# Even mixer of a two-layer encoder step: scan fronts in pinned steps, Toeplitz blocks in column tiles, a shorter warm-up

## The chip, the cores and the metric

One of the eight cores of a Trainium2 chip. The time is device microseconds from launch to end. Engines: PE (TensorE, matmuls), DVE (VectorE), ACT (ScalarE), POOL (GpSimd), and SP (SyncE), which here only issues DMAs. Each works off its own list of instructions in order and waits on semaphores for the others.

## What is computed

A step of a trunk of two layers over 512 prompt frames and 32 sample frames, 1024 features, f32. Layer 0 has the even mixer: a short gated convolution (A) beside a state space model with complex diagonal (B), both from one projection; layer 1 has attention and spatial gating. Each layer ends in a ConvFFN and a gated embedding. Cut to the even mixer:

```python
z = hn @ W['w_even_in'][j]
gb, gc, xa, u = jnp.split(z, [A_WIDTH, 2 * A_WIDTH, 3 * A_WIDTH], axis=-1)
yc, new_hist = causal_dwconv(gc * xa, hist, W['w_conv_a'][j])
ya = gb * yc
yb, nr, ni = s5_mixer(u, h0r, h0i, ...)   # scan over time, 32 groups x 64 states, then
                                          # y = Re(c h) + d*u; g = gelu(y); g * sigmoid(g @ w_glu)
y = jnp.concatenate([ya, yb], axis=-1) @ W['w_even_out'][j]
```

## The kernel before

Activations stand with features on partitions: 8 tiles of 128 features by 544 columns, in two halves of 256 and 288 columns. Every f32 weight and activation is split into a high and a low part (`wh`, `wl`, `Xh`, `Xl`), so that a product of a 128x128 block is three passes (L131 to L133), and a job (`mm_job`) over eight blocks of K is 24 passes, some 3 us. `prefetch` (L92) keeps four weight units loaded ahead: a DMA on SP, `wh` on ACT (L107), `wl` on DVE (L108). `phase` (L166) runs the jobs of a projection, and after each job calls `run(rate)`, which advances the first generator in `tasks` by `rate` steps (`yield`s); a step that yields True ends that call. The result of a job is consumed `lag` jobs later (`drain`), which frees its PSUM buffer; there are four.

The order of each engine's list is laid out when the kernel is built, by a planner that takes the instructions in the order in which the program writes them, but lets one pass ahead that it estimates to be ready sooner.

`mixer_even` (L518) has two phases. The first makes `u` (four units, `c_u`), with norms and `discretize` beside it (rotations `E`, powers `pw`). The second makes A's three parts (`c_a`: 12 units, two halves, so 24 jobs, two steps a job, lag 2), with `scan` beside it. `scan` (L897) is B in chunks: time is cut in blocks of four frames, M = 137 block columns, and the 16 group pairs go two at a time through eight fronts.

- `prep_g(ch)` (L802): builds `G` for four group pairs on ACT and DVE (one step), transposes it on PE into `Bm` (a second).
- `prep_c` (L780): the output matrices `Cm` for the powers 0 to 4, on DVE (L789, L791), in `Tm`'s space as scratch, then zeroes `Tm`.
- `prep_t(ch)` (L831): the Toeplitz blocks inside a block of four frames, `tp` (L837), four group pairs side by side on 32 partitions; copies into `Tm` (L840, L842), and three DMAs on SP for the shifted copies (L845).
- `front(s)` (L852): input products `v` on PE, rotation (L867 to L870), a scan along time (L875) whose coefficients ACT writes into `sp` (L872), rotation back (L877 to L879). `rt`, `rg`, `sp` and `G` come from one pool of four buffers.
- `back(s)` (L883): output products from `sp` and `Tm` on PE, GELU on ACT (L894).
- `shuffle` (L917): 16 DMAs on SP that bring two column groups back to feature order (L924).

The order in `scan` is `back(s-2)`, `front(s)`, then a preparation; a front is one step. Its 32 steps are all plain. After the phase `GG` is made of the shuffled result (L977, L978), and eight products with `w_glu` follow, then the output projection. Ahead of everything PE runs nine matmuls on zeros (L218).

Of the kernel before, what the change touches and what calls it, by code (L numbers as in the profile page):

```python
# [24 lines left out]
M = 137  # L25
# [15 lines left out]
PC["_n"] = 0  # L41
for _n, _w in (("g_mix_pre", 16), ("g_mix_post", 16), ("g_ffn_pre", 16), ("g_ffn_post", 16),
               ("conv_a", 12), ("hist_a", 8), ("a_re", 16), ("a_im", 16),
               ("log_dt", 16), ("st_re", 16), ("st_im", 16), ("d", 16), ("b_forget", 1),
               ("g_gmlp", 4), ("conv_f", 264)):
    _pc(_n, _w)
NPRM = PC["_n"]
NPRM0 = PC["conv_f"][0]

NCST = 128 + 128 + 32  # L50


def units():
# [18 lines left out]
def trunk_kernel(ctx: ExitStack, tc: tile.TileContext, A: dict):  # L72
    nc = tc.nc
    vec, act, pool_e, pe = nc.vector, nc.scalar, nc.gpsimd, nc.tensor
# [132 lines left out]
    cst = const.tile([128, NCST], F32, tag="cst", name="cst")  # L207
    ident = cst[:, 0:128]
    mask_p = cst[:, 128:256]
    mask_s = cst[:, 256:288]  # L210
    ones = const.tile([128, 1], F32, tag="ones", name="ones")
    vec.memset(ones, 1.0)
    mhalf = const.tile([128, 4], F32, tag="mhalf", name="mhalf")
    zero = const.tile([128, 8], F32, tag="zero", name="zero")
    vec.memset(zero, 0.0)
    warm = mm.tile([128, 512], F32, tag="mm", name="warm")
    for _ in range(9):
        pe.matmul(warm[:, 0:256], zero[:, 0:1].to_broadcast([128, 128]), zero[:, 0:1].to_broadcast([128, 256]),  # L218
                  start=True, stop=True)
    act.activation(mhalf, zero[:, 0:4], AF.Gelu_apprx_tanh)  # L220
# [2 lines left out]
    def P(name, j=0, n=1):  # L223
        o, _ = PC[name]
        return prm[:, o + j:o + j + n]
# [292 lines left out]
    def mixer_even(h):  # L518
        ms = ExitStack()
        s5 = ms.enter_context(tc.tile_pool(name="s5", bufs=1))  # L520
# [259 lines left out]
        def prep_c():  # L780
            ct = Tm.rearrange("p (n i a x) c -> p n i a (x c)", n=2, i=2, a=2)
            ct = ct.rearrange("p n i a (q c) -> p n i a q c", q=16)
            for tau in range(5):
                src = raw[:, 0]
                if tau:
                    t = ct[:, tau % 2]
                    for i in range(2):
                        p_ = pw[:, tau, i][:, None, :, None].to_broadcast([128, 2, 16, 16])
                        vec.tensor_tensor(t[:, i], raw[:, i], p_, op=OP.mult)  # L789
                    src = t[:, 0]  # L790
                    vec.tensor_tensor(src, src, t[:, 1], op=OP.add)  # L791
                for g in range(2):
                    s = slice(g * 64, g * 64 + 64)
                    act.activation(Cm[s, :, :, tau, g * 16:g * 16 + 16], src[s], AF.Copy)
                if tau % 2 == 0:
                    yield
            act.activation(Tm.rearrange("p q s -> p (q s)"), zero[:, 0:1].to_broadcast([128, 2048]), AF.Copy)
            yield

        g3 = {}  # L800

        def prep_g(ch):  # L802
            q0 = 4 * ch
            G = pt([128, 2, 4, 4, 32], "G")
            g3[ch] = s5.tile([128, 2, 4, 32], F32, tag="g3", name="g3", bufs=2)
            act.activation(G.rearrange("p a b c d -> p (a b c d)"),
                           zero[:, 0:1].to_broadcast([128, 1024]), AF.Copy)
            for g in range(2):
                s = slice(g * 64, g * 64 + 64)
                act.activation(G[s, :, :, 3, g * 16:g * 16 + 16], bb[s, 0, ch], AF.Copy)  # L810
            act.activation(g3[ch], G[:, :, :, 3], AF.Copy)
            t = [s5.tile([128, 8, 3, 16], F32, tag="gt", name="gt", bufs=2) for _ in range(2)]
            for i in range(2):
                p_ = pg[:, i, q0:q0 + 4][:, None, :, :, None].to_broadcast([128, 2, 4, 3, 16])
                b_ = bb[:, i, ch][:, :, :, None].to_broadcast([128, 2, 4, 3, 16])
                vec.tensor_tensor(t[i].rearrange("p (r q) j c -> p r q j c", r=2), b_, p_, op=OP.mult)
            vec.tensor_tensor(t[0], t[0], t[1], op=OP.add)
            for g in range(2):
                s = slice(g * 64, g * 64 + 64)
                o = G[s, :, :, 0:3, g * 16:g * 16 + 16].rearrange("p r q j c -> p (r q) j c")  # L820
                act.activation(o, t[0][s], AF.Copy)
            yield
            for r in range(2):
                ps = aux.tile([128, 512], F32, tag="y", name="tb", bufs=2)
                for i in range(4):
                    pe.transpose(ps[:, i * 128:i * 128 + 128],
                                 G[:, r, i].rearrange("p j c -> p (j c)"), ident)
                act.activation(Bm[:, r, q0:q0 + 4].rearrange("p q s -> p (q s)"), ps, AF.Copy)
            yield

        def prep_t(ch):  # L831
            q0 = 4 * ch
            G = g3.pop(ch)
            ps = aux.tile([128, 512], F32, tag="y", name="tp", bufs=2)
            for i in range(4):
                for r in range(2):
                    pe.matmul(ps[0:32, i * 128:i * 128 + 128], G[:, r, i],  # L837
                              Cm[:, r, q0 + i, 0:4].rearrange("p t c -> p (t c)"), start=(r == 0), stop=(r == 1))
            pv = ps[0:32].rearrange("p (q s) -> p q s", q=4)
            act.activation(Tm[0:32, q0:q0 + 4, 32:128], pv[:, :, 32:128], AF.Copy)  # L840
            for i in range(4):
                vec.scalar_tensor_tensor(Tm[0:32, q0 + i, 0:32], ident[0:32, 0:32], P("d", q0 + i)[0:32],  # L842
                                         pv[:, i, 0:32], op0=OP.mult, op1=OP.add)
            for j in range(1, 4):
                nc.sync.dma_start(Tm[j * 32:j * 32 + 32, q0:q0 + 4, j * 32:128], Tm[0:32, q0:q0 + 4, 0:128 - j * 32])  # L845
            yield


# [3 lines left out]
        def front(s):  # L852
            q0 = 2 * s
            U4 = UV["U4"]
            ps = aux.tile([128, 2, 512], F32, tag="v", name="v")
# [8 lines left out]
            cf = sp[:, 2:4].rearrange("p a i m -> p (a i m)")[:, 0:4 * M]  # L864
            cv = cf.rearrange("p (r i m) -> p r i m", r=2, i=2)
            t4 = t.rearrange("p e r (q m) -> p e r q m", q=2)
            vec.tensor_tensor(t, v[:, None].to_broadcast([128, 2, 2, 2 * M]), e, op=OP.mult)  # L867
            vec.tensor_tensor(g[:, 0], t4[:, 0, 0], t4[:, 1, 1], op=OP.add)
            vec.tensor_tensor(g[:, 1], t4[:, 0, 1], t4[:, 1, 0], op=OP.subtract)
            vec.tensor_copy(g[:, 0:2, :, 128], P("st_re", 0, 32).rearrange("p (r q) -> p r q", r=2)[:, :, q0:q0 + 2])  # L870
            for i in range(2):
                act.activation(cv[:, :, i], seg[:, None].to_broadcast([128, 2, M]), AF.Copy, scale=K_["mag4"][:, q0 + i:q0 + i + 1])  # L872
            pool_e.memset(sp[:, 0:2, :, 0:1], 0.0)
            g_ = g.rearrange("p (x r) i m -> p x (r i m)", x=2)
            vec.tensor_tensor_scan(g_[:, 1], cf, g_[:, 0], 0.0, op0=OP.mult, op1=OP.add)  # L875
            w_ = g_[:, 1].rearrange("p (r x) -> p r x", r=2)
            vec.tensor_tensor(t, w_[:, None].to_broadcast([128, 2, 2, 2 * M]), e, op=OP.mult)  # L877
            vec.tensor_tensor(sp[:, 0, :, 1:M + 1], t4[:, 0, 0], t4[:, 1, 1], op=OP.subtract)
            vec.tensor_tensor(sp[:, 1, :, 1:M + 1], t4[:, 0, 1], t4[:, 1, 0], op=OP.add)  # L879
            act.activation(so[:, q0:q0 + 2].rearrange("p q (r c) -> p r q c", r=2), sp[:, 0:2, :, 128:138:9], AF.Copy)  # L880
            SP[s] = sp
# [13 lines left out]
                           AF.Gelu_apprx_tanh)  # L895

        def scan():  # L897
            yield from prep_g(0)
            yield from prep_g(1)
            for s in range(10):  # L900
                if s >= 2:
                    back(s - 2)
                    yield
                if s == 5:
                    shuffle(True, (0, 1))
                if s < 8:
                    front(s)
                    yield
                    if s == 0:
                        yield from prep_c()  # L910
                    if s % 2 == 0:
                        yield from prep_t(s // 2)
                    elif s < 5:
                        yield from prep_g(s // 2 + 2)
            shuffle(True, (2, 3))

        def shuffle(back_, fs):  # L917
# [458 lines left out]
def host_arrays(inp):  # L1376
# [51 lines left out]
    def put(name, a):  # L1428
        o, n = PC[name]
        prm[:, o:o + n] = a  # L1430
# [19 lines left out]
    put("d", np.tile(f["s5_d"][0].reshape(16, 32).T, (4, 1)))  # L1450
# [6 lines left out]
    cst[:, 128:256] = np.where(i[None, :] <= i[:, None], 0.0, NEG)  # L1457
    j = np.arange(32)
    cst[:, 256:288] = np.where(j[None, :] <= (i % 32)[:, None], 0.0, NEG)
    A["cst"] = cst  # L1460

    def gpc(v):
# [56 lines left out]
```

## Time and profile before

| | us |
|---|---|
| median of 3 runs | 1391.64 |
| lowest and highest | 1391.41, 1392.94 |
| profiled execution | 1392.53 |
| its span, first to last instruction | 1390.8 |

| engine | busy us | share of the span |
|---|---|---|
| PE matmul | 1367.2 | 98% |
| DVE | 935.7 | 67% |
| ACT | 657.4 | 47% |
| POOL | 198.3 | 14% |

The times are read from one execution of the program; the even mixer takes the first 170 us of it. A busy PE may still lose time, since matmuls are pipelined: what counts is how far apart their starts are. The profile's page gives the sums; the stretches, the waits and the timelines tell where in the kernel they arise.

### The profile page before, as it was taken

How to read it: one execution, taken by the hardware profiler on the slowest of the kernel's cores; microseconds unless marked ns; L12 is line 12 of the kernel's file. 1: busy time of each engine (PE TensorE's matmuls, PEld its weight loads, DVE VectorE, ACT ScalarE, POOL GpSimd, SP SyncE). 2: the span in 40 equal slices, each digit the busy share in tenths (PEclk: the TensorE clock that was granted, in tenths of full speed). 3: DMA queues.
4: the chain of work that ended last, by engine and by line, in shares of the span. 5: the costliest groups of instructions: out<-in, count | busy, mean ns of one | idle time of the engine just before them, and what ended most of it. 6: DMA issues, size and time to landing. Idle time of an engine off the chain costs nothing.

```text
span 1390.8 us, 27437 instructions
## 1 busy us (share of the span) xinstructions
PE 1367.2 (98%) x10859; PEld 1344.2 (97%) x10859; DVE 935.7 (67%) x1968; ACT 657.4 (47%) x1314; POOL 198.3 (14%) x621
## 2 busy tenths in 40 slices
PE   8899999999999999999999999999999999999998
PEld 8798999999999999999998998999999999999998
DVE  9998738983477546868655555479843676368682
ACT  6653545543344223445547755465433343234451
POOL 1000000431022201300131100012320123013000
PEclk9999999999999999999999999999999999999999
DMA  6322352232312231331332332331223123313321
GB/s 199 94 67 63 117 184 77 77 96 72 122 62 86 97 122 39 105 113 53 99 94 70 117 109 64 108 107 62 92 92 122 46 92 107 99 50 94 100 73 50
DMA packets 49376, 128.26 MB, mean 92 GB/s; under 512 B 8368, under 2 KB 19896, under 8 KB 48992
## 3 DMA queue, kind: packets, MB, share of 16 engines
q1 hardware_dynamic: 47456, 124.35, 28.0%
q0 software_dynamic: 1792, 2.17, 0.7%
q8 instruction: 85, 1.39, 0.4%
q14 instruction: 43, 0.35, 0.1%
HBM read 116.93 MB, written 4.76 MB: 88 GB/s over the span
## 4 chain that ended last, share of the span: by engine, by line
PE 87%; DVE 8%; ACT 2%; SPq 1%; DMA 1%; issue 1%; POOL 0%; ACTq 0%; DVEq 0%
PE ps L131 27%; PE ps L133 27%; PE ps L132 27%; DVE wl L108 1%; SPq L924 1%; PE av L1254 1%; PE rp L307 1%; DVE Xl L327 1%; PE pp L1243 1%; DVE rg L875 1%; DVE rt L877 1%; ACT wh L107 1%; PE sc L1230 1%; DVE y L338 0%; DMA h<-in_x 0%
## 5 line engine op out<-in xcount | busy, mean ns | idle before, releaser
L131 PE MATMUL ps<-Xh,wh 128*128 128x256 f32 (+1 forms) x2512 | 728.1, 290 | 1.8 <-ACT wh L107 1.1
L133 PE MATMUL ps<-Xh,wl 128*128 128x256 f32 (+1 forms) x2512 | 725.5, 289 | 2.0 <-DVE wl L108 2.0
L132 PE MATMUL ps<-Xl,wh 128*128 128x256 f32 (+1 forms) x2512 | 725.6, 289 | 0.8 <-DVE Xl L327 0.5
L131 PEld LDWEIGHTS ps<-Xh,wh 128*128 128x128 f32 x2512 | 473.9, 189 | 4.4 <-ACT wh L107 1.6
L132 PEld LDWEIGHTS ps<-Xl,wh 128*128 128x128 f32 x2512 | 474.7, 189 | 3.0 <-DVE Xl L327 1.2
L133 PEld LDWEIGHTS ps<-Xh,wl 128*128 128x128 f32 x2512 | 473.0, 188 | 2.5 <-DVE wl L108 2.4
L108 DVE TENSOR_TENSOR wl<-raw,wh 128x1024 fp32r<-128x1024 f32 (+2 forms) x214 | 256.9, 1201 | 151.3 <-ACT wh L107 149.5
L107 ACT ACTIVATE wh<-raw 128x1024 fp32r<-128x1024 f32 (+2 forms) x214 | 222.1, 1039 | 248.3 <-PE ps L132 232.9
L131 PE MATMUL ps<-gh,wh 128*128 128x288 f32 (+1 forms) x704 | 203.5, 289 | 0.0
L133 PE MATMUL ps<-gh,wl 128*128 128x288 f32 (+1 forms) x704 | 203.4, 289 | 0.0
L132 PE MATMUL ps<-gl,wh 128*128 128x288 f32 (+1 forms) x704 | 202.5, 288 | 0.0
L132 PEld LDWEIGHTS ps<-gl,wh 128*128 128x128 f32 x704 | 133.5, 190 | 0.0
L131 PEld LDWEIGHTS ps<-gh,wh 128*128 128x128 f32 x704 | 133.0, 189 | 0.0
L133 PEld LDWEIGHTS ps<-gh,wl 128*128 128x128 f32 x704 | 132.9, 189 | 0.0
L278 ACT ACTIVATE t<-U,prm 128x256 f32<-128x256 f32 (+1 forms) x176 | 90.4, 517 | 71.0 <-DVE U L413 67.5
L279 DVE SCALAR_TENSOR_TENSOR t<-U,prm,t 128x256 f32<-128x256 f32 (+1 forms) x176 | 87.2, 498 | 34.9 <-ACT t L278 34.7
L413 DVE TENSOR_TENSOR U<-ps,rB 128x256 f32<-128x256 f32 (+1 forms) x176 | 76.6, 437 | 23.9 <-PE ps L133 19.8
L280 DVE SCALAR_TENSOR_TENSOR t<-U,prm,t 128x256 f32<-128x256 f32 (+1 forms) x176 | 87.5, 501 | 4.5
L416 POOL COPY hca<-U 128x2 f32<-128x2 f32 x88 | 24.3, 277 | 366.2 <-DVE U L413 366.1
L423 ACT ACTIVATE t<-t 128x288 f32<-128x288 f32 (+1 forms) x88 | 37.7, 429 | 81.6 <-DVE t L280 81.5
L439 DVE TENSOR_TENSOR y<-y,ps 128x256 f32<-128x256 f32 (+1 forms) x64 | 27.9, 436 | 62.0 <-PE ps L133 62.0
L429 ACT ACTIVATE gh<-t 128x288 fp32r<-128x288 f32 (+1 forms) x88 | 37.4, 425 | 67.3 <-DVE t L427 67.3
(272 smaller groups left out, 1376.7 us busy)
## 6 DMA issues: line engine op xcount, KB each, us to landing
raw<-in_w_up SPq DMA_DIRECT2D x88, 512.0 KB, 3.4
raw<-in_w_down SPq DMA_DIRECT2D x32, 512.0 KB, 3.4
raw<-in_w_odd_in SPq DMA_DIRECT2D x21, 512.0 KB, 3.6
raw<-in_w_gate SPq DMA_DIRECT2D x16, 512.0 KB, 4.0
raw<-in_w_even_in SPq DMA_DIRECT2D x15, 512.0 KB, 3.7
raw<-in_w_down SPq DMA_DIRECT2D x16, 384.0 KB, 3.1
raw<-in_w_even_out SPq DMA_DIRECT2D x8, 512.0 KB, 4.0
raw<-in_w_odd_out SPq DMA_DIRECT2D x8, 512.0 KB, 3.5
```

What stands on the lines that cost most here:

```text
L107: act.activation(wh[:, k], raw[:, k], AF.Copy)
L108: vec.tensor_tensor(wl[:, k], raw[:, k], wh[:, k], op=OP.subtract)
L131: pe.matmul(ps[:, :n], wh[:, k0 + k, :], h_, start=(i == 0), stop=False)
L132: pe.matmul(ps[:, :n], wh[:, k0 + k, :], l_, start=False, stop=False)
L133: pe.matmul(ps[:, :n], wl[:, k0 + k, :], h_, start=False, stop=(i == last))
L278: act.activation(t, v[2], AF.Copy, scale=w(2))
L279: vec.scalar_tensor_tensor(t, v[1], w(1), t, op0=OP.mult, op1=OP.add)
L280: vec.scalar_tensor_tensor(t, v[0], w(0), t, op0=OP.mult, op1=OP.add)
L413: vec.tensor_tensor(block_view(U, half)[2], like(ps, half), like(rB[half], half), op=OP.mult)
L423: act.activation(t, t, AF.Gelu_apprx_tanh)
L429: act.activation(gh[:, f - f0], g, AF.Copy)
L439: vec.tensor_tensor(yk, yk, ps, op=OP.add)
```

## The change

- A front becomes a generator of three pieces: rotation, scan with the first half of the rotation back, and the rest. `pin` (`tc.keep_in_program_order`) holds an instruction behind the one that the program writes just before it on its engine; it is put on DVE's operations of `prep_c` and `prep_g` and on four of a front.
- `scan` takes four steps a front and advances one list of preparations (`side`) between them; `left` says how many of these must be done ahead of a front. `back(s-2)` now stands behind the scan of front `s`. `back(6)` and `back(7)` are the last two.
- `prep_c` yields after each power from 1 on; the first step of `prep_g` yields True.
- `prep_t` writes the four blocks of a chunk to four column tiles of PE, on 128 partitions of one PSUM tile; two copies into `ts_` take them all, and 16 DMAs carry them into `Tm`, the diagonal included. `d` is laid out to fit (4 columns for 16), and `cst` has 32 columns more.
- The warm-up has seven matmuls for nine.

```diff
-    for _ in range(9):
+    for _ in range(7):
...
             for i in range(2):
...
-                        vec.tensor_tensor(t[:, i], raw[:, i], p_, op=OP.mult)
+                        pin(vec.tensor_tensor(t[:, i], raw[:, i], p_, op=OP.mult))
                     src = t[:, 0]
-                    vec.tensor_tensor(src, src, t[:, 1], op=OP.add)
+                    pin(vec.tensor_tensor(src, src, t[:, 1], op=OP.add))
...
-                if tau % 2 == 0:
+                if tau:
                     yield
...
-            yield
+            yield True
...
-            for i in range(4):
-                for r in range(2):
-                    pe.matmul(ps[0:32, i * 128:i * 128 + 128], G[:, r, i],
-                              Cm[:, r, q0 + i, 0:4].rearrange("p t c -> p (t c)"), start=(r == 0), stop=(r == 1))
-            pv = ps[0:32].rearrange("p (q s) -> p q s", q=4)
-            act.activation(Tm[0:32, q0:q0 + 4, 32:128], pv[:, :, 32:128], AF.Copy)
-            for i in range(4):
-                vec.scalar_tensor_tensor(Tm[0:32, q0 + i, 0:32], ident[0:32, 0:32], P("d", q0 + i)[0:32],
-                                         pv[:, i, 0:32], op0=OP.mult, op1=OP.add)
-            for j in range(1, 4):
-                nc.sync.dma_start(Tm[j * 32:j * 32 + 32, q0:q0 + 4, j * 32:128], Tm[0:32, q0:q0 + 4, 0:128 - j * 32])
+            ts_ = s5.tile([128, 128], F32, tag="ts", name="ts")
+            for r in range(2):
+                for i in range(4):
+                    pe.matmul(ps[32 * i:32 * i + 32, 0:128], G[:, r, i],
+                              Cm[:, r, q0 + i, 0:4].rearrange("p t c -> p (t c)"), start=(r == 0), stop=(r == 1),
+                              tile_position=(0, 32 * i))
+            vec.scalar_tensor_tensor(ts_[:, 0:32], eye4, P("d", ch), ps[:, 0:32], op0=OP.mult, op1=OP.add)
+            act.activation(ts_[:, 32:128], ps[:, 32:128], AF.Copy)
+            for j in range(4):
+                for i in range(4):
+                    nc.sync.dma_start(Tm[j * 32:j * 32 + 32, q0 + i, j * 32:128],
+                                      ts_[32 * i:32 * i + 32, 0:128 - j * 32])
...
             pool_e.memset(sp[:, 0:2, :, 0:1], 0.0)
+            yield
             g_ = g.rearrange("p (x r) i m -> p x (r i m)", x=2)
-            vec.tensor_tensor_scan(g_[:, 1], cf, g_[:, 0], 0.0, op0=OP.mult, op1=OP.add)
+            pin(vec.tensor_tensor_scan(g_[:, 1], cf, g_[:, 0], 0.0, op0=OP.mult, op1=OP.add))
             w_ = g_[:, 1].rearrange("p (r x) -> p r x", r=2)
             vec.tensor_tensor(t, w_[:, None].to_broadcast([128, 2, 2, 2 * M]), e, op=OP.mult)
-            vec.tensor_tensor(sp[:, 0, :, 1:M + 1], t4[:, 0, 0], t4[:, 1, 1], op=OP.subtract)
+            yield
+            pin(vec.tensor_tensor(sp[:, 0, :, 1:M + 1], t4[:, 0, 0], t4[:, 1, 1], op=OP.subtract))
...
+            side = [prep_c(), prep_t(0), prep_g(2), prep_t(1), prep_g(3), prep_t(2), prep_t(3)]
+            left = [0, 0, 1, 3, 5, 5, 6, 6]
+
+            def beside():
+                while side:
+                    try:
+                        return next(side[0])
+                    except StopIteration:
+                        side.pop(0)
+
+            for s in range(8):
+                while 7 - len(side) < left[s]:
+                    yield beside()
+                f = front(s)
+                next(f)
+                yield
+                yield beside()
+                next(f)
+                yield
                 if s >= 2:
                     back(s - 2)
...
+                x = beside()
+                if s == 6:
                     shuffle(True, (0, 1))
...
+                yield x
+                next(f, None)
+            yield
+            while side:
+                beside()
+            back(6)
+            yield
+            back(7)
             shuffle(True, (2, 3))
```

## Rows read from the trace of the kernel before

**Rows 1.** The page: busy time and instructions by engine; the chain, by engine.

```profile
PE 1367.2 (98%) x10859; PEld 1344.2 (97%) x10859; DVE 935.7 (67%) x1968; ACT 657.4 (47%) x1314; POOL 198.3 (14%) x621
...
PE 87%; DVE 8%; ACT 2%; SPq 1%; DMA 1%; issue 1%; POOL 0%; ACTq 0%; DVEq 0%
```

**Rows 2.** Stretches: length; busy PE, PEld, DVE, ACT, POOL; clock; DMA; GB/s.

```profile
38.40:60.00 21.60, 20.31 (x167) 20.01 (x166) 21.60 (x56) 15.06 (x31) 0.11 (x1) 1.00 0.48 129
...
60.00:80.00 20.00, 15.41 (x107) 14.06 (x105) 20.00 (x37) 11.96 (x19) 0.11 (x1) 0.83 0.11 33
...
100.00:120.00 20.00, 17.22 (x138) 16.20 (x137) 14.25 (x28) 8.64 (x22) 0.30 (x3) 1.00 0.22 60
...
140.00:156.10 16.10, 16.10 (x126) 16.10 (x126) 11.60 (x23) 7.76 (x17) 0.00 (x0) 1.00 0.37 112
```

**Rows 3.** PE's waits, 44 to 157 us: total us, times, longest.

```profile
PE tp L837 <- ACT Cm L794: 4.5, 1, 4.5
PE tb L826 <- ACT G L821: 2.9, 3, 1.3
PE yp L893 <- DMA Tm<-Tm: 1.8, 1, 1.8
PE yp L891 <- DVE sp L878: 1.4, 1, 1.4
```

**Rows 4.** Stretches, L837 alone: length; busy PE, PEld; clock; DMA; GB/s.

```profile
66.15:69.73 3.58, 3.54 (x16) 2.60 (x16) 0.50 0.00 0
83.70:85.57 1.87, 1.86 (x16) 1.67 (x16) 1.00 0.00 0
```

**Rows 5.** Timeline of PE, 755 us: start, us, instruction, count.

```profile
755.01 0.88 PE L1254 MATMUL av<-pT,VT 128*64 128x128 f32 x12
755.82 0.33 PE L1230 MATMUL sc<-KA,QA 128*128 128x128 f32 x1
```

**Rows 6.** Timeline of PE at its longest wait.

```profile
66.19 0.63 PE L837 MATMUL tp<-Cm,g 128*32 128x128 f32 x2 [4.48 <-ACT Cm L794]
```

**Rows 7.** DVE by line, 44 to 137 us: count, busy us, mean ns.

```profile
L867 DVE TENSOR_TENSOR rt<-v,E 128x1096 f32<-128x1096 f32 x8 | 10.3, 1289 | 0.0
...
L789 DVE TENSOR_TENSOR Tm<-Bm,pw 128x512 f32<-128x512 f32 x8 | 5.4, 683 | 0.0
...
L878 DVE TENSOR_TENSOR sp<-rt 128x274 f32<-128x274 f32 x8 | 3.5, 436 | 0.1
...
L941 DVE TENSOR_TENSOR gct<-ps,rB 128x256 f32<-128x256 f32 (+1 forms) x7 | 3.0, 423 | 0.0
...
L108 DVE TENSOR_TENSOR wl<-raw,wh 128x1024 fp32r<-128x1024 f32 x7 | 8.5, 1214 | 0.0
```

**Rows 8.** Timeline of SP's queue: start, us, transfer, count.

```profile
101.25 0.33 SPq L106 DMA_DIRECT2D raw<-in_w_even_in  x1
...
112.92 1.88 SPq L845 DMA_DIRECT2D Tm<-Tm  x3
...
132.02 10.31 SPq L924 DMA_DIRECT2D UUh<-UUh  x16
```

**Rows 9.** DMA issues: transfer, count, size, us to landing.

```profile
UUh<-UUh SPq DMA_DIRECT2D x32, 34.2 KB, 1.9
```

**Rows 10.** Timelines of ACT and PE at the end of the scan.

```profile
136.71 0.40 ACT L894 ACTIVATE UUh<-yp 128x274 f32<-128x274 f32 x1 [1.08 <-PE yp L893]
...
145.13 0.66 ACT L977 ACTIVATE GG<-UUh 128x548 fp32r<-128x548 f32 x1 [3.21 <-DMA UUh<-UUh]
...
156.05 0.28 PE L131 MATMUL ps<-GG,wh 128*128 128x274 f32 x1
```

**Rows 11.** Timelines of PE and DVE at the start.

```profile
1.03 6.52 PE L218 MATMUL warm<-zero 128*128 128x256 f32 x18 [1.03 <-DVE zero L215]
...
13.46 0.38 PE L133 MATMUL ps<-Xh,wl 128*128 128x256 f32 x1 [0.86 <-DVE wl L108]
...
7.93 2.65 DVE L327 SCALAR_TENSOR_TENSOR Xl<-h,prm,Xh 128x256 fp32r<-128x256 f32 x6 [0.32 <-ACT Xh L323]
```

More of the change, by code (lines that the diff above doesn't have):

```diff
@@ L43 @@
                ("conv_a", 12), ("hist_a", 8), ("a_re", 16), ("a_im", 16),
-               ("log_dt", 16), ("st_re", 16), ("st_im", 16), ("d", 16), ("b_forget", 1),
+               ("log_dt", 16), ("st_re", 16), ("st_im", 16), ("d", 4), ("b_forget", 1),
                ("g_gmlp", 4), ("conv_f", 264)):
@@ L48 @@
 NPRM0 = PC["conv_f"][0]
-NCST = 128 + 128 + 32
+NCST = 128 + 128 + 32 + 32
 def units():
@@ L210, in trunk_kernel @@
     mask_s = cst[:, 256:288]
+    eye4 = cst[:, 288:320]
     ones = const.tile([128, 1], F32, tag="ones", name="ones")
@@ L794, in prep_c @@
                     act.activation(Cm[s, :, :, tau, g * 16:g * 16 + 16], src[s], AF.Copy)
-                if tau % 2 == 0:
+                if tau:
                     yield
             act.activation(Tm.rearrange("p q s -> p (q s)"), zero[:, 0:1].to_broadcast([128, 2048]), AF.Copy)
-            yield
         g3 = {}
+        pin = tc.keep_in_program_order
         def prep_g(ch):
@@ L815, in prep_g @@
                 b_ = bb[:, i, ch][:, :, :, None].to_broadcast([128, 2, 4, 3, 16])
-                vec.tensor_tensor(t[i].rearrange("p (r q) j c -> p r q j c", r=2), b_, p_, op=OP.mult)
-            vec.tensor_tensor(t[0], t[0], t[1], op=OP.add)
+                pin(vec.tensor_tensor(t[i].rearrange("p (r q) j c -> p r q j c", r=2), b_, p_, op=OP.mult))
+            pin(vec.tensor_tensor(t[0], t[0], t[1], op=OP.add))
             for g in range(2):
@@ L821, in prep_g @@
                 act.activation(o, t[0][s], AF.Copy)
-            yield
+            yield True
             for r in range(2):
@@ L866, in front @@
             t4 = t.rearrange("p e r (q m) -> p e r q m", q=2)
-            vec.tensor_tensor(t, v[:, None].to_broadcast([128, 2, 2, 2 * M]), e, op=OP.mult)
+            pin(vec.tensor_tensor(t, v[:, None].to_broadcast([128, 2, 2, 2 * M]), e, op=OP.mult))
             vec.tensor_tensor(g[:, 0], t4[:, 0, 0], t4[:, 1, 1], op=OP.add)
@@ L899, in scan @@
             yield from prep_g(1)
-            for s in range(10):
+            side = [prep_c(), prep_t(0), prep_g(2), prep_t(1), prep_g(3), prep_t(2), prep_t(3)]
[15 more added lines that the diff above has]
+                yield
                 if s >= 2:
                     back(s - 2)
-                    yield
-                if s == 5:
+                x = beside()
+                if s == 6:
                     shuffle(True, (0, 1))
[L906 to L914, printed above, removed]
+                yield x
[6 more added lines that the diff above has]
+            back(7)
             shuffle(True, (2, 3))
@@ L1449, in host_arrays @@
     put("st_im", gp(f["state_ssm_im"][0, 0]))
-    put("d", np.tile(f["s5_d"][0].reshape(16, 32).T, (4, 1)))
+    put("d", f["s5_d"][0].reshape(4, 128).T)
     prm[:8, PC["b_forget"][0]] = f["b_forget"][0]
@@ L1459, in host_arrays @@
     cst[:, 256:288] = np.where(j[None, :] <= (i % 32)[:, None], 0.0, NEG)
+    cst[:, 288:320] = np.tile(np.eye(32), (4, 1))
     A["cst"] = cst
```

## The prediction

> **What bounds the kernel now.** I read the page first: the share of busy time and the chain of work that ended last. TensorE (PE) is busy for 98% of the span and makes up 87% of the chain [rows 1]. So a microsecond counts only if PE's stream gets shorter or one of its waits does. Next I read busy time by stretch, for the even mixer's second phase alone (38.4 to 156.1 us) [rows 2]. There VectorE (DVE) is busy for all of 21.6 us and then for all of 20 us, while PE loses 4.6 us of the second stretch and its granted clock falls to 0.83, a mean of full (2.4 GHz) and half (1.2 GHz). In the last stretch, 140 to 156.1, PE is busy throughout. So two engines are full in turn: DVE early, PE late. Last I read PE's waits in the phase: 4.5 us for `Cm`, 2.9 us in three waits for `G`, 1.8 us for a transfer into `Tm`, 1.4 us for the last front, 10.6 us in all [rows 3]. That is what better order could return; it is also all of it.
>
> The profiled execution took 1392.53 us, of which 1390.8 are its span; the median of the runs is 1391.64. The other 1.7 us lie around the span and are not touched, so I work out a difference inside the span and put it on the median.
>
> **Toeplitz blocks in column tiles.** Before, a block of four takes 16 passes one after the other, 1.86 us, and 3.54 us in the one case where the clock stood at 0.50 [rows 4]. After, four 32-column tiles take the same passes side by side. The trace has this with two tiles: 12 passes of L1254, also 128 columns of f32, fill 0.81 us from their start to the next instruction [rows 5], so a pair costs about 0.1 and leaving the group 0.2. Four side by side in four rounds: 4 x 0.11 + 0.2 = 0.64. Saved: 4 x (1.86 - 0.64) = 4.9 us, on PE, which is the bound late in the phase. Bounds: only two ever overlap, 8 x 0.1 + 0.2 = 1.0, saves 3.4; none overlap, 0; a price below 0.64 isn't to be had from these rows. I take 4.9, since the pair row shows full overlap.
>
> **Where a run's steps end.** A step of `scan` is advanced twice after each of the phase's 24 jobs, and a step that yields True ends that turn. Two steps of `discretize` are left over at the phase's start. Before, `scan` has 32 steps, none True: 34 steps, so `back(7)` stands after job 17. After, I count 42 steps, four of them True (one in each `prep_g`): `back(7)` stands after job 23. This carries most of what follows. Six jobs of about 3 us that lay behind the scan now lie among it.
>
> **The waits for G, 2.9 us.** `prep_g` now ends its turn, so one whole job always lies between DVE's part and the transposes. I take 2.5 back. Bounds: 0 (the buffer of `G` may be what is late, and it comes from the same four as the fronts') to 2.9.
>
> **The wait for Cm, 4.5 us, and the clock.** The wait itself is a row; the half clock behind it cost 3.54 - 1.86 = 1.7 in that block alone [rows 3, 4]: 6.2 together. PE sat from 61.7 to 66.19 [rows 6]. After, `prep_t(0)` stands two jobs later; a pass of a late job is 0.128 (126 in 16.1 us), a job of 24 is 3.1 [rows 2], so PE would come at 67.9. But power 3 of `prep_c`, the last that this block needs, is now pinned behind front 0, the first half of front 1, and three jobs' consumption. From the rows on DVE: two long operations and smaller ones of the second front's start 1.3 + 2 x 0.44 + 0.1, the end of the first 0.9, six operations of 0.43 for three jobs 2.6, one weight split 1.2, and four operations of `prep_c` that ran ahead of the first front before, 2.7 [rows 7]: about 9.7 us more. Of the last 2.7 I take 1.8 off, since the first front starts sooner without them, as soon as its rotations are done. So `Cm` is ready near 66.1 + 7.9 = 74.0. PE would wait 6.1; the planner can put the ninth job (3.1) in front. Left: 3.0 + 1.7 of clock = 4.7, a gain of 1.5. Bounds: everything goes (6.2) to 3 lost. It is not free that DVE work is pinned: whatever is queued behind a pinned scan on DVE, the consumption of jobs among it, holds PE's PSUM buffers.
>
> **Toeplitz transfers.** Three transfers a block become 16, all on SP's queue, and the diagonal block now goes by SP too; 12 become 64. Before, three take 1.88, and 16 of the shuffle 10.31, so 0.63 each; a weight load, one run a partition, takes 0.33 [rows 8]. The new ones have one run a partition like the load, but 32 partitions like the copies: I take 0.45, with 0.33 and 0.63 as ends. Landing takes 1.9 more [rows 9]. A block is then whole 16 x 0.45 + 1.9 + 0.5 for the two copies = 9.6 us after its matmuls. `back(0)` follows `prep_t(0)` by two jobs (6.2) and the 16 passes of a front and of `prep_g` (1.9, as 16 passes of rows 4), 8.1 us: a wait of 1.5, nearly the present one of 1.8, so 0 here (bounds: 1.8 gained at 0.33, as 7.7 is under 8.1; at 0.63 a wait of 4.4, 2.6 lost). SP's weight loads queue behind, but a weight is loaded four units ahead, so 7 to 10 us stay hidden; without that cover each late unit would stop PE for what is missing. `ts_` is a single buffer: the two writes of `prep_t(3)`, one job after `prep_t(2)`, wait for all of its 16 transfers, on DVE and ScalarE, with a front's scan queued behind. DVE's sixteen small operations become four, a gain of 2 us on an engine with some idle by then: nothing. The last front's wait of 1.4: 0.5 back (bounds 1.4 to -3).
>
> In a sentence apart, the Trainium skill, page "DMA: Bandwidth & Descriptors" (Specifications), gives about 0.6 us as the first-byte latency of the queues that SP uses, and its rules for kernel authors advise one 128-partition transfer over several on parts; the 0.63 rows agree with the first and the 0.33 row does not; by 0.6 the wait above would be 3.9 and the term a loss of about 2.1 instead of 0.
>
> **The end of the scan.** Before, `back(7)` ends at 136.7, its GELU at 137.1, the last transfers are issued by 142.33, the first conversion that needs them starts at 145.13, and PE turns to `GG` at 156.05 without a wait [rows 8, 10]: 19.3 us of jobs cover it, 6.3 jobs, where the written order leaves seven. After, one job (3.1) is left. `back(6)` and `back(7)` now stand in one turn, so all 16 transfers, 10.3, are still to issue: 0.4 + 10.3 + 1.9, less the 1.4 of `back(7)`'s own twelve passes, plus 0.7 for the conversion, so 11.9 from `back(7)`'s end to the first product that needs it. Cover: job 24, 3.1; the first half of the inputs of four products, which don't depend on those transfers, 24 passes, 3.1; what slides behind the waiting backs, 0.7 job as before, 2.2. Left 3.5, and as the clock fell in a wait of 4.5 before, 1.7 again: 5.2 lost. Bounds: 0 (two jobs more slide) to 11.9 - 3.1 + 1.7 = 10.5.
>
> **Warm-up.** Two matmuls less are 4 of 18 passes. Behind them the first job waits on other things: `Xl` comes off DVE until 10.6, and the second job waits for `wl` until 13.46 [rows 11]. Those don't move, so 0. Bounds: 4/18 x 6.5 = 1.4 gained; lost, if the clock opens later, about the same.
>
> **Sum.** -4.9 - 2.5 - 1.5 + 0 - 0.5 + 5.2 + 0 = -4.2. The few columns less of `prm` and more of `cst` go in loads that nothing here waits for. 1391.64 - 4.2 = **1387.4 us**.
>
> **Rivals.**
> 1. *The end is covered*: waits shift jobs behind `back(7)`, or the scan finishes sooner, and the 5.2 shrinks to 0: -9.4, 1382.2 us. For it: before, the planner already slid jobs behind waiting products. Against: DVE was full early, and six jobs' work now stands ahead of the last front on it.
> 2. *A swap*: tiles overlap in pairs only (+1.5) and the end costs 7 (+1.8): -0.9, 1390.7 us. Here the change does, in time, not what it says: one wait for another.
> 3. *SP decides* (slower): at 0.63 a transfer `back(0)` costs 2.6 more, and `prep_t(3)` holds DVE for about 10.1 + 1.9 - 4 = 8 us behind `ts_`. The fronts are one chain on DVE, so I let 6 of them reach the end: -4.2 + 2.6 + 6 = +4.4, 1396.0 us. For it: SP's 0.63 rows. Against: between 100 and 120 us DVE is busy for 14.3 of 20 [rows 2], so it can make some of that up. It decides from about 0.5 us a transfer.
>
> **How the numbers follow.** Forecast 0.40, rival 1 0.22, rival 2 0.19, rival 3 0.19. What a measurement of this kernel can tell from no change is about 0.2%, 2.8 us: the border is 1388.9, close to the forecast, of which I count 0.30 as faster and 0.10 as the same. Faster 0.30 + 0.22 = 0.52; same 0.10 + 0.19 = 0.29; slower 0.19. The forecast's own range is 1384.5 to 1390.5. The range reaches into rivals 1 and 3: 1381 to 1396; half of either's spread lies outside.
>
> **What would show it.** Each Toeplitz block's 16 passes within 0.5 to 0.7 us of PE (else term one is wrong). PE's waits for `G` below 1 us. A wait for `Cm` or for a PSUM buffer near 67 to 75 us, with the clock at half behind it. SP issuing the new transfers at 0.33 to 0.63 each, and whether `back(0)` waits for `Tm`. At the end, an idle PE ahead of the `GG` products for some 4 us, released by the shuffle's last transfers: if there is none, rival 1; if 8 or more, rival 2 or 3. The prediction fails above all if the planner's order moves `back(7)` far from job 23.

## The result and the profile after

The changed kernel takes 1400.49 us (median of 5 runs, 1398.02 to 1402.45), the kernel before 1391.64 in the same comparison (1389.78 to 1393.72). The ratio is 1.0059, 95% interval 1.0041 to 1.0077: 0.6% slower. The profiled execution took 1398.38 us with a span of 1396.6; it is one of the quicker ones, so its trace shows 5.8 us of span more than before, not the whole 8.85. Matched matmul by matmul from the end, the two traces are 7.3 us apart at 185 to 220 us, where the even mixer is done. Then 1.6 us of this go, and over the 1,140 us that follow 5.7 stay, within 0.2. The 1.6 us are no work of the change: in the profiled execution of the kernel before, PE ran the same jobs at half clock at 231 to 234.5 us, behind a wait of 0.5 us that both kernels have. A stretch of each (columns as in rows 2), before and after:

```profile
232.00:234.00 2.00, 2.00 (x11) 2.00 (x11) 2.00 (x7) 1.29 (x3) 1.34 (x4) 0.50 0.00 0
```

```profile
238.00:240.00 2.00, 2.00 (x19) 2.00 (x19) 1.47 (x6) 1.24 (x3) 1.24 (x5) 1.00 0.00 0
```

So the loss arises in the even mixer, and there it is 7.3 us in this pair of traces.

The page's chain, by engine and by line, beside rows 1:

```profile
PE 85%; DVE 8%; SPq 3%; ACT 2%; DMA 2%; issue 1%; POOL 0%; DVEq 0%; ACTq 0%
PE ps L131 27%; PE ps L133 27%; PE ps L132 27%; DVE wl L108 2%; SPq L846 2%; PE av L1276 1%; SPq L946 1%; DVE Xl L328 1%; PE rp L308 1%; DMA raw<-in_w_glu 1%; PE pp L1265 1%; ACT wh L107 1%; DVE rg L878 1%; PE sc L1252 1%; DVE rt L880 0%
```

SP's share went from 1 to 3%, and the line that brought it is L846: the 64 new transfers are themselves on the path that sets the end, and with them the two loads of `w_glu` (at 112.2 and 145.5 us).

Stretches (columns as in rows 2). PE loses its time in three places: 60 to 80 (3.9 us, 4.6 before), 120 to 140 (2.2, 1.4 before), and above all 140 to 156.1 (7.1), where it was busy throughout before:

```profile
60.00:80.00 20.00, 16.13 (x127) 15.03 (x126) 19.92 (x34) 11.04 (x20) 0.10 (x1) 0.91 0.17 53
...
120.00:140.00 20.00, 17.85 (x142) 17.47 (x142) 16.95 (x29) 7.86 (x20) 0.21 (x2) 1.00 0.11 25
140.00:156.10 16.10, 9.03 (x71) 8.80 (x69) 12.36 (x21) 6.08 (x15) 0.10 (x1) 0.88 0.41 126
...
156.00:162.00 6.00, 5.59 (x25) 5.62 (x26) 5.79 (x12) 2.50 (x6) 0.00 (x0) 0.50 0.17 40
```

The last of these rows shows the clock at its lower level (1.2 GHz) behind that loss: PE works at half speed from 156.4 to 162.6 us.

PE's waits, 44 to 178 us (rows 3 is the same view of before): total us, times, longest.

```profile
PE yp L895 <- DVE sp L882: 9.1, 2, 7.4
PE v L860 <- DVE rt L869: 2.8, 2, 2.4
PE tb L827 <- ACT G L822: 2.7, 3, 1.1
PE yp L895 <- ACT Cm L795: 1.5, 1, 1.5
PE ps L131 <- ACT GG L999: 1.1, 1, 1.1
PE yp L897 <- DMA Tm<-ts: 0.9, 1, 0.9
```

With two of 0.4, and 1.8 in front of the output projection behind 178 us, they make 20.7 us, against 10.6 before plus 0.8 at the same place behind 157 us, so 9.3 more. Work at the half clock costs 2.6 more: 1.7 behind the wait at 70 us and 3.1 here, against 2.2 before. The column tiles give 4.9 back (below). 9.3 + 2.6 - 4.9 = 7.0 of the 7.3 us; 0.3 is unexplained.

The Toeplitz blocks alone (L839), columns as in rows 4. The last row holds two blocks:

```profile
70.50:73.00 2.50, 1.08 (x16) 0.59 (x16) 0.50 0.02 7
98.90:99.70 0.80, 0.64 (x16) 0.38 (x16) 1.00 0.00 0
111.40:112.60 1.20, 1.13 (x32) 0.75 (x32) 1.00 0.28 34
```

So 0.64 us where it was 1.86, at full clock: four tiles do run side by side.

SP's queue (rows 8): start, us, transfers.

```profile
111.32 0.53 SPq L106 DMA_DIRECT2D raw<-in_w_even_in  x1
112.22 0.33 SPq L106 DMA_DIRECT2D raw<-in_w_glu  x1
113.20 10.92 SPq L846 DMA_DIRECT2D Tm<-ts  x16
124.22 3.20 SPq L946 DMA_DIRECT2D UUh<-UUh  x5
127.51 10.06 SPq L846 DMA_DIRECT2D Tm<-ts  x16
137.62 7.84 SPq L946 DMA_DIRECT2D UUh<-UUh  x11
145.50 0.58 SPq L106 DMA_DIRECT2D raw<-in_w_glu  x1
```

16 transfers take 10.06 us, 0.63 each, and from 113.2 to 145.5 the queue is never free for a weight. What that does to VectorE, first at 125 us, then at 150, and to ScalarE at 149 (timelines: start, us, instruction, the idle time before it and what ended it):

```profile
125.66 0.25 DVE L842 SCALAR_TENSOR_TENSOR ts<-cst,prm,tp 128x32 f32<-128x32 f32 x1 [2.07 <-DMA Tm<-ts]
125.83 1.29 DVE L878 TENSOR_TENSOR_SCAN rg<-sp,rg 128x548 f32<-128x548 f32 x1
...
146.17 0.43 DVE L871 TENSOR_TENSOR rg<-rt 128x274 f32<-128x274 f32 x1
150.34 1.23 DVE L108 TENSOR_TENSOR wl<-raw,wh 128x1024 fp32r<-128x1024 f32 x1 [3.74 <-ACT wh L107]
151.49 0.17 DVE L872 COPY rg<-prm 128x4 f32<-128x4 f32 x1
...
151.92 1.29 DVE L878 TENSOR_TENSOR_SCAN rg<-sp,rg 128x548 f32<-128x548 f32 x1
```

```profile
149.25 1.06 ACT L107 ACTIVATE wh<-raw 128x1024 fp32r<-128x1024 f32 x1 [4.68 <-DMA raw<-in_w_glu]
150.22 1.06 ACT L874 ACTIVATE sp<-seg,sb 128x274 f32<-128x274 f32 x2
```

At 125 us a scan stands behind the write of the last block's sums, which waits for the third block's transfers to leave `ts_`. At 146 us the last front has its rotated inputs, but the weight that SP began to load at 145.5 is in its way on both engines. On VectorE its `wl` stands ahead of the front's remaining steps. On ScalarE its `wh` stands ahead of the scan's coefficients (L874), so these come at 151.3. The scan starts at 151.9; without both halves of the split it could have by about 147 (an estimate: 146.17 + 0.43 + 0.17 by these rows). PE's timeline, the wait for it:

```profile
156.41 1.25 PE L895 MATMUL yp<-sp,Cm 128*128 128x137 f32 x4 [7.38 <-DVE sp L882]
```

### The profile page after: what moved, and what is told of

Read it like the earlier page. It is cut to its first block, busy times and chain, and to the rows that moved or that the text cites. A ratio compares the mean times of both kernels' runs of the same rounds, so it can differ in the third digit from the quotient of the medians.

```text
span 1396.6 us, 27494 instructions
## 1 busy us (share of the span) xinstructions
PE 1363.4 (98%) x10855; PEld 1339.7 (96%) x10855; DVE 933.3 (67%) x1956; ACT 653.3 (47%) x1314; POOL 197.3 (14%) x621
## 4 chain that ended last, share of the span: by engine, by line
PE 85%; DVE 8%; SPq 3%; ACT 2%; DMA 2%; issue 1%; POOL 0%; DVEq 0%; ACTq 0%
PE ps L131 27%; PE ps L133 27%; PE ps L132 27%; DVE wl L108 2%; SPq L846 2%; PE av L1276 1%; SPq L946 1%; DVE Xl L328 1%; PE rp L308 1%; DMA raw<-in_w_glu 1%; PE pp L1265 1%; ACT wh L107 1%; DVE rg L878 1%; PE sc L1252 1%; DVE rt L880 0%
```

## The experiments

Theory A: SP's queue decides. The 64 transfers at 0.63 us make late what stands behind them or waits for their buffer. Theory B: the order decides, because the last fronts now stand behind nearly all jobs and nothing covers the end. Theory C: the pins hold the last scan in the wrong place. Differences in microseconds below are the ratio's interval times 1391.6; the changed kernel is at +8.2 (5.7 to 10.7) on that scale.

| kernel | median us | ratio to before (95%) | difference us |
|---|---|---|---|
| changed kernel | 1400.5 | 1.0059 (1.0041 to 1.0077) | +8.2 |
| tiles_only | 1394.6 | 1.0024 (1.0015 to 1.0033) | +3.3 |
| order_only | 1394.7 | 1.0018 (1.0009 to 1.0027) | +2.5 |
| after_pool | 1391.7 | 1.0007 (0.9998 to 1.0016) | +1.0 |
| after_nopin | 1400.3 | 1.0067 (1.0054 to 1.0079) | +9.3 |
| after_wpool | 1398.1 | 1.0047 (1.0034 to 1.0060) | +6.5 |
| after_ts2 | 1398.1 | 1.0043 (1.0030 to 1.0055) | +6.0 |
| after_ts2w | 1393.8 | 1.0016 (1.0007 to 1.0025) | +2.2 |
| after_shpool | 1395.9 | 1.0029 (1.0018 to 1.0040) | +4.0 |
| after_early | 1398.2 | 1.0046 (1.0034 to 1.0058) | +6.4 |
| early_pool | 1389.0 | 0.9974 (0.9964 to 0.9984) | -3.6 |
| tiles_pool | 1386.8 | 0.9961 (0.9949 to 0.9973) | -5.4 |
| tiles_pool_w7 | 1387.1 | 0.9965 (0.9951 to 0.9979) | -4.9 |

### One part of the change at a time

**tiles_only** is the kernel before with the changed `prep_t` and its constants (that part of the diff above), nothing else. Its core:

```
+                              tile_position=(0, 32 * i))
...
+            for j in range(4):
+                for i in range(4):
+                    nc.sync.dma_start(Tm[j * 32:j * 32 + 32, q0 + i, j * 32:128],
```

> The kernel before with the column tiles alone (16 transfers a block on SP; old order of the scan, nine warm-up matmuls). Theory A, SP's queue decides: 64 transfers at 0.63 us stand on SP here too, so weight loads and the buffer of the tile sums come late in any order; -4.9 us for the tiles and 7 to 10 us lost behind SP: 1393 to 1397 us. Theory B, the order decides (last fronts after job 23, uncovered): here the last front stands where it stood, so only the tiles show: 1386.0 to 1388.5 us. In both a block's 16 passes take 0.64 us.

Measured 1394.6, +3.3 us: theory A's range. The order is the old one, the tiles save what they should, and the kernel is slower. First PE's two longest waits (44 to 178 us), then SP's queue:

```profile
PE yp L895 <- DMA Tm<-ts: 5.5, 3, 3.7
PE tp L839 <- ACT Cm L795: 4.5, 1, 4.5
```

```profile
125.46 10.06 SPq L846 DMA_DIRECT2D Tm<-ts  x16
...
148.49 0.53 SPq L106 DMA_DIRECT2D raw<-in_w_glu  x1
```

The last block's transfers start at 125.5 behind a shuffle, so the products that read it wait 3.7 us, and PE runs at half clock from 135.3 to 138.7. The second `w_glu` load comes at 148.5, later than in the changed kernel, and there PE doesn't wait for it: it starts on `GG` at 156.28, as before at 156.05. In the kernel before this load starts at 142.4, only 3 us ahead of the changed kernel's; the last front was done by 135 there. A late load alone isn't the harm, then; it needs a front behind it, and it is the new order that puts one there.

**order_only** is the changed kernel with the `prep_t` of before: three transfers a block.

```
-            ts_ = s5.tile([128, 128], F32, tag="ts", name="ts")
...
+            for j in range(1, 4):
+                nc.sync.dma_start(Tm[j * 32:j * 32 + 32, q0:q0 + 4, j * 32:128], Tm[0:32, q0:q0 + 4, 0:128 - j * 32])
```

> The changed kernel with the Toeplitz blocks of before (three transfers a block on SP), so the new order, the pins and the shorter warm-up are left. Theory A, SP's queue decides: the loads of weights are early again, nothing of the even_out weights stands in front of the last scan on DVE, PE's wait of 7.4 us at 149 us goes; the end still has one job of cover, so 1388 to 1393 us. Theory B, the order decides: the last front still stands behind job 23, the wait of 7.4 us and the half clock stay, and the tiles' 4.9 us are missing: 1403 to 1406 us.

Measured 1394.7, +2.5 us: above A's range, far under B's. A row of SP's queue, and then the longest of PE's waits, show why:

```profile
127.53 0.53 SPq L106 DMA_DIRECT2D raw<-in_w_glu  x1
```

```profile
PE ps L131 <- ACT GG L998: 3.9, 1, 3.9
...
PE v L859 <- DVE rt L868: 2.4, 1, 2.4
PE yp L894 <- ACT GG L998: 1.1, 1, 1.1
```

The load is 18 us sooner and the wait of 7.4 us for the last scan is gone. What is left is the uncovered end: 3.9 us in front of the `GG` products, 1.1 beside it, and 1.7 of half clock behind (162 to 168 us). So B holds too, for a part.

**after_nopin** replaces the pin by a function that does nothing. In a front the pin is on three operations (L869, L878, L882), not four as written above.

```
-        pin = tc.keep_in_program_order
+        pin = lambda x: x
```

> The changed kernel without its pins (the planner may move the fronts' and the preparations' operations on DVE again; steps, transfers and warm-up as changed). Theory C, the pins hold the last scan behind the late weight split on DVE, or the split in front of the scan: without them the wait of 7.4 us goes and the time is 1391 to 1395 us. Theories A and B both leave it: 1398 to 1402 us.

Measured 1400.3, +9.3 us: theory C falls. The wait for the last scan shrinks to 1.7 us, yet nothing is won. The planner now puts the last scan at 144.4 us, ahead of the late split; SP issues the second `w_glu` load at 148.8, and what is late now is `GG`, made of what the shuffles bring (141.8 to 148.8 and 154.1 to 164.8). The waits that stand in its place (the one of 4.8 us is at 69 us, ahead of all 64 transfers):

```profile
PE ps L131 <- ACT GG L999: 7.7, 2, 4.0
PE v L860 <- DVE rt L869: 5.5, 2, 4.8
...
PE yp L895 <- DVE sp L882: 1.7, 1, 1.7
```

The longest wait of a trace is where the lateness surfaced, not necessarily its cause: the late split in front of the last scan is one outlet of a late queue, not the price itself.

### Taking the queue apart

**after_pool** issues the 64 transfers on GpSimd.

```
-                    nc.sync.dma_start(Tm[j * 32:j * 32 + 32, q0 + i, j * 32:128],
+                    nc.gpsimd.dma_start(Tm[j * 32:j * 32 + 32, q0 + i, j * 32:128],
```

> The changed kernel with the 64 transfers into the Toeplitz blocks issued by GpSimd (POOL) in place of SyncE (SP); all else as changed. GpSimd does 1 us of work in this phase. Theory A, SP's queue decides: the weight loads no longer stand behind them; the wait of 7.4 us goes, what is left of the end costs 0 to 5 us: 1385 to 1391 us, with the blocks still landing no earlier if a transfer costs GpSimd more than 0.63 us. Theory B, the order decides: 1398 to 1402 us, as the changed kernel.

Measured 1391.7, +1.0 us (-0.3 to 2.2): just above A's range, far from B's. Some 7 of the 8.2 us hang on which queue issues these transfers. A block's 16 on GpSimd's timeline, and then the load on SP:

```profile
100.20 7.84 POOL L846 DMA_DIRECT2D Tm<-ts  x16 [10.45 <-DVE ts L842]
```

```profile
126.34 0.54 SPq L106 DMA_DIRECT2D raw<-in_w_glu  x1
```

GpSimd issues one in 0.49 us, so it isn't slower than SP, and the second `w_glu` load starts at 126.3 in place of 145.5. The Trainium skill, page "DMA: Bandwidth & Descriptors" (Issuing engines are not separate DMA queues), says that issuing on several engines saves only the time that a sequencer takes to initiate a transfer, and that this is usually small relative to the transfer itself. The trace agrees that it is this time that is saved, and disagrees on its size: a transfer holds SP for 0.63 us and lands 1.8 us after its issue, and the 64 hold it for 64 x 0.63 = 40 us, worth 7 us here.

**after_wpool** leaves the transfers on SP and moves 20 weight loads instead.

```
-                nc.sync.dma_start(raw[:, k], A[name][idx][:, k])
+                (nc.gpsimd if 12 <= len(loaded) < 32 else nc.sync).dma_start(raw[:, k], A[name][idx][:, k])
```

> The changed kernel with 20 weight loads (the last four of w_even_in, w_glu, w_even_out and the first six behind) issued by GpSimd in place of SyncE; the 64 transfers into the Toeplitz blocks and the shuffle stay on SyncE. Theory A1, the late weight loads are what SP's queue costs: the loads no longer stand behind the transfers, the wait of 7.4 us for the last scan goes, and the time comes near the 1391.7 us of the run with the transfers on GpSimd: 1391 to 1394 us. Theory A2, the transfers themselves and the single buffer behind them are what is late (block sums held on DVE until all 16 have landed, 0.63 us each): the time stays at 1397 to 1401 us.

Measured 1398.1, +6.5 us: A2, the loads alone are not it. The second `w_glu` load is issued at 124.5 and the wait of 7.4 us does go, as A1 said; PE waits 1.7 us for the last front and 3.5 for one before it. The time doesn't follow. VectorE's timeline shows the other delay, grown from 2.07 to 4.34 us, with the same scan behind it:

```profile
128.96 0.25 DVE L842 SCALAR_TENSOR_TENSOR ts<-cst,prm,tp 128x32 f32<-128x32 f32 x1 [4.34 <-DMA UUh<-UUh]
129.12 1.29 DVE L878 TENSOR_TENSOR_SCAN rg<-sp,rg 128x548 f32<-128x548 f32 x1
```

The profile names a transfer of the shuffle as what released it, though the write needs only the third block's transfers to have left `ts_`, and the last of these is issued by 125.4. What held it beyond them is open.

**after_ts2** gives the last block's sums another buffer.

```
-            ts_ = s5.tile([128, 128], F32, tag="ts", name="ts")
+            if ch == 3:
+                ts_ = s5.tile([128, 8, 3, 16], F32, tag="gt", name="ts", bufs=2).rearrange("p a b c -> p (a b c)")
+            else:
+                ts_ = s5.tile([128, 128], F32, tag="ts", name="ts")
```

> The changed kernel with a second buffer for the last block's sums (ts_ of prep_t(3) takes a buffer that prep_g has left), so that VectorE needn't wait at 125 us until the third block's 16 transfers have landed, with a scan queued behind. All transfers stay on SP. Theory A2a, the single buffer is the main price of the transfers: 3 to 6 us back, 1395 to 1398 us. Theory A2b, what is late is the queue itself (shuffle and weight loads behind 64 transfers): within 1 us of the changed kernel, 1399 to 1402 us.

Measured 1398.1, +6.0 us: between the two ranges, and on the interval not to be told from no change. The trace tells more. VectorE no longer waits for the buffer, SP's queue then runs 48 transfers in a row, and PE again waits 7.4 us. The last scan itself has run at 140.4 here; the weight's split stands ahead of one product of that front, of 0.44 us (L885, right behind the split in VectorE's list):

```profile
112.98 20.88 SPq L849 DMA_DIRECT2D Tm<-ts  x32
133.96 10.80 SPq L949 DMA_DIRECT2D UUh<-UUh  x16
144.86 0.53 SPq L106 DMA_DIRECT2D raw<-in_w_glu  x1
```

```profile
149.78 1.23 DVE L108 TENSOR_TENSOR wl<-raw,wh 128x1024 fp32r<-128x1024 f32 x1 [5.82 <-ACT wh L107]
```

```profile
151.51 0.80 PE L898 MATMUL yp<-sp,Cm 128*128 128x137 f32 x2 [7.44 <-DVE sp L885]
```

**after_ts2w** has both edits, the one of after_ts2 and the one of after_wpool.

> Second buffer and the 20 weight loads on GpSimd, both; transfers and shuffle stay on SP. With the loads alone on GpSimd it took 1398.0 us and VectorE then stood 4.3 us in front of the last block's sums. If the two delays hide each other, as theory A now says (each alone leaves the other in place), both together give more than the sum of the single ones: 1392 to 1395 us, near the 1391.7 us with the transfers on GpSimd. If what is late is the shuffle behind the transfers: 1396 to 1398 us.

Measured 1393.8, +2.2 us: inside the range. 6.0 us of the 8.2 are back, where the singles gave 1.7 and 2.2. That the sum of the singles is less isn't certain from these intervals; that each delay was still there when only the other was taken away is in their traces. PE's wait for the last scan is 1.3 us. What is left is the end:

```profile
PE ps L131 <- ACT GG L1002: 5.3, 1, 5.3
```

**after_shpool** issues the scan's shuffle on GpSimd; transfers and loads stay on SP.

```
-                    nc.sync.dma_start(a if back_ else b, b if back_ else a)
+                    (nc.gpsimd if back_ else nc.sync).dma_start(a if back_ else b, b if back_ else a)
```

> The changed kernel with the 32 transfers of the shuffle that brings the scan's outputs back issued by GpSimd in place of SP; Toeplitz transfers and weight loads stay on SP. If the shuffle's place in the queue is the price (it stands on SP from 124 to 145 us between transfers and ahead of the even_out loads, and at 152 to 166 us at the end): the loads come 8 us sooner, the wait of 7.4 us goes, and the end's 32 transfers start as their inputs come: 1392 to 1396 us. If the Toeplitz transfers alone are: 1398 to 1401 us.

Measured 1395.9, +4.0 us: the upper end of the first range, so half of the loss. The second `w_glu` load starts at 126.0, between the third block and the fourth, and PE's longest wait for a scan falls to 1.6 us. So of the queue's three kinds of work the 64 transfers give back 7.2 of the 8.2 us when they are moved off, the shuffle 4.2, and the loads 1.7, which the intervals can't tell from nothing. They share one queue; the transfers are what the change added to it.

### The end, and what is best

**after_early** leaves out one yield of each front, 8 steps in all, so that the last front is asked for some four jobs sooner. **early_pool** has that edit and the one of after_pool.

```
                 next(f)
-                yield
                 yield beside()
```

> The changed kernel with one of a front's yields left out, so that a front's first part and the preparation beside it share a step: 8 steps fewer, back(7) behind about job 19 in place of 23, three jobs of about 3 us more behind the scan; the transfers stay on SP. Theory A, SP's queue decides: the fronts are asked for sooner but the 64 transfers and the loads behind them need the same 40 us; 1397 to 1402 us. Theory B, the uncovered end decides: 5 to 8 us back, 1392 to 1396 us.

> Both: the changed kernel with the 64 transfers on GpSimd and the 8 steps fewer. With the transfers on GpSimd alone it took 1391.7 us, and PE then waited 2.4 us for the last front and 2.2 us for the shuffle at the end, with the clock at half for 7 us there. Theory: what is left of the loss is the uncovered end, so three jobs more of cover take 4 to 6 us off: 1386 to 1388 us. Rival: the fronts are bound by DVE, not by when they are asked for; 1390 to 1393 us.

With the transfers on SP: 1398.2, +6.4 us, as theory A expects: asking sooner helps little while the queue is full. PE waits 0.8 us at most for a front there, but 6.1 for `GG`. With them on GpSimd: 1389.0, between the theory's range and its rival's; 2.7 us under after_pool by the medians and 4.6 by the ratios, short of the 4 to 6 expected at the median. PE waits 0.3 us for `GG` there, where it waited 2.2: the end is covered. The price of late fronts is real; it is the smaller part.

**tiles_pool** is tiles_only with the edit of after_pool, the transfers on GpSimd; **tiles_pool_w7** has seven warm-up matmuls as well.

> The kernel before with the column tiles alone, their 64 transfers issued by GpSimd (0.49 us each in the run of the changed kernel with them there). Against the same kernel with the transfers on SP (1394.6 us). Theory A: nothing stands in front of the weight loads and of the shuffle, the wait of 3.7 us for the last block and its half clock go; the tiles' 4.9 us remain as a gain, less 0 to 2 us of waits for Tm: 1386 to 1389 us. Rival: the column tiles save nothing that reaches the end, because another wait takes their place: 1391 to 1394 us.

> The order of before with column tiles and the transfers on GpSimd (1386.8 us), and seven warm-up matmuls in place of nine. The prediction took the warm-up at nothing, bounds 1.4 either way. At nothing: 1386 to 1388 us. If the first jobs start sooner by what is left out: 1385 to 1386 us; if the clock opens later: 1388 to 1389 us.

Measured 1386.8, -5.4 us (-7.1 to -3.8), inside the range, and faster than both kernels: the one part of the change that is worth its while, with the old order and its transfers off SP. PE's waits (44 to 178 us):

```profile
PE tp L839 <- ACT Cm L795: 4.5, 1, 4.5
...
PE yp L895 <- issue: 1.6, 1, 1.6
```

```profile
126.53 0.47 PE L895 MATMUL yp<-UUh,Tm 128*128 128x137 f32 x2 [1.59 <-issue]
```

No wait is put down to a block or a front here; the wait for `Cm` of before stands as it was. The 1.6 us for which the profile names no releaser stand in front of a product that reads `Tm`, while GpSimd issues the last block's transfers (118.5 to 126.3 us): probably what is left of the 3.7 us that the last block cost on SP. The warm-up: 1387.1 against 1386.8, no difference that these runs can tell, within some 2 us.

## Why the prediction was wrong

It forecast 1387.4 us (1381 to 1396) and gave slower 0.19. The time is 4.5 us above the range. The term that failed is the one for the Toeplitz transfers: 0 in the sum, with bounds of 1.8 gained and 2.6 lost. Moved off SP, the same transfers give back 7.2 us in the new order (after_pool) and 8.7 in the old one (tiles_pool against tiles_only). Its third rival had the right engine, SP, and the wrong waits behind it; the forecast took the wrong price for a transfer and the wrong cover.

- **The step that failed first: 0.45 us a transfer.** The bounds were 0.33 and 0.63, and the middle was taken. The nearer rows were those of the shuffle and of the old Toeplitz transfers (SBUF to SBUF): 0.63, and 0.63 it is. The first-byte latency of about 0.6 us that the prediction sets beside these rows is another quantity, so that they agree confirms nothing: a transfer that holds SP for 0.63 lands 1.8 us after its issue. By the prediction's own sum this price alone makes 2.6 us, so it is not the larger part.
- **The second: "a weight is loaded four units ahead, so 7 to 10 us stay hidden".** Each block was costed by itself. On SP blocks three and four and the shuffle follow one another for 32 us. And a late weight did not stop its own job: its split on VectorE and ScalarE stood in front of the last scan. tiles_only shows that a late weight with no front behind it costs nothing at that place, and after_nopin that with the split out of the scan's way PE waits for `GG` instead, behind the shuffles in the same queue. The prediction had asked what is queued behind a pinned scan, not what a scan is queued behind.
- **`ts_`.** Rival 3 had VectorE held 8 us behind it; it was 2.1 here and 4.3 in after_wpool. Right place, too large; a buffer of its own gave back 2.2 us, not clear of nothing (after_ts2).
- **`back(0)` and `Tm`.** It waited 0.9 us, against 1.5 forecast and 4.4 if a transfer cost 0.63: it came to its product with `Tm` only at 89.5 us, 11.5 behind its first with `Cm`, with other work in between. That bound of the rival was too high.
- **Rival 3's size.** +4.4 us forecast with the gains of the order in it, +8.2 measured. Most of these gains weren't there, and the half clock behind the long wait was left out: the 3.1 us from 156.4 to 162.6.
- **The tiles: right.** 0.64 us a block, 4.9 saved at full clock; tiles_pool is 5.4 us faster.
- **The waits for G: wrong, at the bound of 0 that was named.** They are 2.7 us (2.9 before). The turn now ends behind VectorE's part, but ScalarE first zeroes the buffer of `G`, and that waits for a front's products on VectorE to leave one of the four shared buffers (4.0 us at the longest), as the bound said it might. ScalarE's waits, 44 to 178 us:

```profile
ACT G L807 <- DVE rt L880: 5.1, 2, 4.0
```

- **The wait for Cm: 1.5 forecast as a gain.** The block no longer waits. In its place PE waits 2.4 us for a PSUM buffer that a front's products hold (`v`), 1.5 for `Cm` in `back(0)`, and works 1.7 us longer at half clock: 5.6 against 6.2, so 0.6 gained. (The 6.2 count the half clock in that block alone; with all of it, the 2.2 above, it is 6.7 and 1.1 gained.) order_only, without the 1.5, gains 2.1.
- **The end of the scan: right in kind, a little small.** 3.5 idle and 1.7 of clock were forecast; order_only has 3.9 and 1.7, and 1.1 beside them. In the changed kernel PE waits only 1.1 us for `GG`, because the wait of 7.4 comes ahead of it.
- **The warm-up: 0, and no run shows otherwise.**

Order and warm-up by the forecast: -2.5 - 1.5 - 0.5 + 5.2 = +0.7; order_only measures +2.5 (1.3 to 3.8). Tiles on SP: forecast -4.9, measured +3.3. The whole error is 12.4 us (+8.2 against -4.2). 8.2 of it show with the tiles alone, and they are the queue's: on GpSimd the same tiles give -5.4. 1.8 show with the order alone. The last 2.4 show only with both (3.3 + 2.5 = 5.8, not 8.2): the wait of 7.4 us, too, is in neither of these two traces.

One thing stays open. On GpSimd the tiles gave -5.4 and the order +2.5, which would make -2.9; both together (after_pool) are at +1.0. In its trace PE waits 2.4 us for the last front, with 3.4 us at half clock behind it, and order_only has neither there. The fronts may bind sooner when PE comes sooner. early_pool, with no wait over 0.4 us for a front's result and -3.6, points that way, but it moves the end's cover too, so no run tells the two apart.

## What to carry to other kernels

When a change multiplies small transfers, price the whole queue that issues them, not each group: write down all that stands on it between two weights, at the price of the nearest row of the same kind. Ask of every operation in a dependent chain what stands ahead of it on its engine, and what that in turn waits for; a delay that is hidden from the matmuls can be in front of a scan, on each engine that feeds it. And before a useful part is given up for its transfers, try them on an engine whose queue is idle: here the same tiles cost 3.3 us on SP and gained 5.4 on GpSimd.

## What the runs showed of the hardware

- A transfer of 32 partitions from SBUF to SBUF takes SP 0.63 us to issue, GpSimd 0.49; on SP one of 4 KB stands for as long as one of 16 KB. A weight load of 512 KB takes SP 0.33, and 0.53 to 0.58 directly behind such transfers.
- Sixteen passes in four column tiles take 0.64 us at full clock and 1.08 at half: a factor of 1.7, not 2.
- The lower clock follows a wait, but not each of like length. Behind the 2.4 us at 70 us in the changed kernel it was 0.61 from 70 to 72 and 0.53 from 72 to 74; in after_wpool, behind 2.4 at 71.7 and 3.0 at 79.5, it stayed at 1.00. So two like waits can differ by the 1.7 us behind them. The kernel before and the changed kernel both end a wait of 0.5 us in front of the same product, at 229.6 and 236.9 us; behind it the clock was 0.50 from 232 to 234 in the first and stayed at 1.00 in the second.
